# Linear attention segments: where the first products, the key turns and the small sample products stand in TensorE's hand-written order

## The chip, the core and the metric

The kernel runs on one core of one Trainium2 chip. The metric is the device time of one execution in microseconds (us). Before the change three timed executions took 1906.51, 1906.85 and 1907.57 us, median 1906.85.

## What is computed

One layer of a streaming encoder, for a prompt of 1024 rows and a sample of 32 rows with shared weights: an input projection, a gated linear attention (GLA), a banded softmax attention, a merge, a convolutional feed-forward part and a gated embedding. The change is in the GLA, which is in the reference

```python
b = jnp.cumsum(ai, axis=2)
decay = jnp.exp(jnp.where(mask, b[:, :, :, None, :] - b[:, :, None, :, :], -jnp.inf))
scores = jnp.einsum('bhic,bhjc,bhijc->bhij', qi, ki, decay)
o = (jnp.einsum('bhij,bhjv->bhiv', scores, vi)
     + jnp.einsum('bhic,bhcv->bhiv', qi * jnp.exp(b), S))
S = (jnp.exp(bl)[..., None] * S
     + jnp.einsum('bhjc,bhjv->bhcv', ki * jnp.exp(bl[:, :, None] - b), vi))
```

for 4 heads with keys of 128 and values of 256 columns, and for the sample from a given state.

## The kernel before

The GLA stage works through 16 **segments**, numbered u = 0 to 15: four per head, each of 256 prompt rows (two blocks of 128). The fourth segment of each head (u = 3, 7, 11, 15) also holds the 32 sample rows. The scores inside a block depend on the decay between two rows, so they are made in levels: level 0 pairs neighbours, level l pairs the two halves of runs of 2 to the l+1 rows, up to level 6, and a diagonal product gives the row with itself. On each level VectorE and ScalarE scale the keys and queries into tile `x`, TensorE multiplies them, and VectorE copies the valid part under a mask into `scores`.

TensorE, VectorE and ScalarE run in the order in which the code is written (a manual schedule); each engine stands until what its next instruction reads is there. Between the small GLA products TensorE has **filler**: the big projections of other heads, cut into units of 24 products of 352 columns (L818 to L820), and each unit into three pieces of 9, 9 and 6. `piece()` puts one piece into TensorE's order, `flush()` then has the finished unit copied out of PSUM, and the first piece of some units also splits the next weights into two halves on ScalarE and VectorE (L235, L236). `need` says after which segment an additional piece is given, so that the units last for the loop.

TensorE's order in one segment of the kernel before, with the lines of before:

- the diagonal products (L1256) and level 0 (L1263), the turn of the weighted keys (L1287, a transpose), one piece
- levels 1 and 2 (L1270, in the sample's segments each followed by the sample's product L1273), one piece
- the products that update the state (L1324, L1327), levels 3 and 4, the turn of the previous segment's outputs (L1408, L1412), one piece
- levels 5 and 6, two pieces
- the turn of the scores (L1278), one piece
- the outputs: old state and scores times values (L1347, L1348 with `scores`, L1348 with `turned`, and L1352, L1353 for the sample), then two or three pieces.

Beside it, the turns of the values (L1184) and the three decay products of the next head (L1064) are spread over the first three segments of a head. ScalarE copies the turned keys (L1292) before the state products can start; VectorE makes the masked copies (L1302, L1306, L1310), and the masked copy into `turned` (L1280) that the last output product reads. The diagonal products of the sample, its level products 1 to 4 and the diagonal products of the blocks are written into one PSUM tile, `dg`. All these products write one of six single PSUM banks.

Of the kernel before, what the change touches and what calls it, by code (L numbers as in the profile page):

```python
# [21 lines left out]
NS = 32  # L22
# [91 lines left out]
def emit(tc, a):  # L114
    nc = tc.nc
    ve, ac, po, pe, dma = nc.vector, nc.scalar, nc.gpsimd, nc.tensor, nc.sync
# [330 lines left out]
    for g, (n, c) in enumerate(PLE):  # L447
        s = chunk(c)
# [255 lines left out]
    B, HA, X, R, S = {}, {}, {}, {}, {}  # L704

    def blocks(t, m):
        return t.rearrange("p (n s) -> p n s", s=2 * m)
# [58 lines left out]
    fill = {"raw": {}, "w": {}, "at": 0, "load": 0, "split": 0, "now": None, "done": []}  # L766
# [26 lines left out]
    def gate_rows(n2):  # L793
        for n in (2 * n2, 2 * n2 + 1):
            GB[n] = tl(bo, [P, T], tag=f"gb{n}") if n2 else evt()
            dma.dma_start(GB[n], d_gb[n])
# [31 lines left out]
    def piece():  # L828
        if fill["now"] is None:
            if fill["at"] == len(units):  # L830
                return
            fill["now"] = unit_parts(*units[fill["at"]]), 0
        parts, n = fill["now"]
        next(parts)
        fill["now"] = (parts, n + 1) if n < 2 else None
        if n == 0:
            i, c = units[fill["at"]]
            if c < 2 and fill["split"] == i + 1 <= FIRST:
                split_half(c)
                if c:  # L840
                    load_tile()
        if n == 2:
            fill["at"] += 1

    def flush():
        for f in fill["done"]:
            f()
        fill["done"].clear()
# [278 lines left out]
    for i in range(len(WORK) + SK + 1):  # L1127
        g, j = divmod(i, NW)
# [14 lines left out]
        n = i - SK - 1  # L1143
# [29 lines left out]
    def head(h):  # L1173
        kq = tl(gp, [P, 2, T], tag="kq", bufs=2)
        HA.setdefault(h, {}).update({"kq": kq, "k": kq[:, 0], "q": kq[:, 1], "vt": tl(gp, [P, 9, 256], tag="vt", bufs=2)})

    def turn_values(h, n):
        g = HA[h]
        cnt = min(2, 9 - n)
        ps = ps_one()  # L1180
        w = P if n < 8 else NS
        for i in range(cnt):
            for j in range(2):
                pe.transpose(ps[:w, i * 256 + j * P : i * 256 + (j + 1) * P], g[f"v{j}"][:, (n + i) * P : (n + i) * P + w], ident)  # L1184
        ac.activation(g["vt"][:w, n : n + cnt], ps[:w, : cnt * 256].rearrange("p (i v) -> p i v", v=256), AF.Copy)

    def seg(u):
        h, s = divmod(u, 4)
        t0, nt = SEGS[s]
        return HA[h], h, s, t0, nt  # L1190
# [51 lines left out]
    def level_bank(u, l):  # L1242
        return R[u]["lo" if l < 4 else "hi"][:, 128 * (l % 4) : 128 * (l % 4) + 128]

    def level_products(u, between):
        g, h, s, t0, nt = seg(u)
        x, k, q, qo = X[u], g["k"], g["q"], g["qo"]
        r = R[u]
        r.update({"dg": ps_one(), "lo": ps_one(), "hi": ps_one()})
        dg = r["dg"]  # L1250
        cnt = (nt + P - 1) // P
        ns = [(t0 // P + i, i * P, P if i < 2 else NS) for i in range(cnt)]
        r["ns"] = ns
        for i, (n, o, w) in enumerate(ns):
            o, m = (P - o, n ^ 1) if i < 2 else (o, n)
            pe.matmul(dg[:w, o : o + w], k[:, n * P : n * P + w], q[:, m * P : m * P + w], start=True, stop=True)  # L1256

        def to(i, l, w):
            return level_bank(u, l)[:w, 64 * i : 64 * i + 64] if i < 2 else dg[:w, 288 + 16 * l : 304 + 16 * l]

        for i, (n, o, w) in enumerate(ns):
            m = n ^ 1 if i < 2 else n
            pe.matmul(to(i, 0, w), k[:, n * P : n * P + w], qo[:, m * 64 : m * 64 + w // 2], start=True, stop=True)  # L1263
        r["to"] = to
        for l in range(1, 7):
            if l == 4:
                score_copies(u, range(-1, 4))
            if l % 2:
                between[l // 2]()
            pe.matmul(level_bank(u, l), x[:, l - 1, 0:P], x[:, l - 1, P : 2 * P], start=True, stop=True)  # L1270
            if len(ns) > 2 and 2 << l <= NS:
                xs = x[:, l - 1, 256:nt]
                pe.matmul(to(2, l, NS), xs, blocks(xs, 1 << l)[:, :, 1 << l :], start=True, stop=True)  # L1273

    def score_turn(u):
        r = R[u]
# [5 lines left out]
    def key_turns(u):  # L1282
        g, h, s, t0, nt = seg(u)
        r = R[u]
        kp = r["kp"] = ps_one()
        for n, o, w in r["ns"]:
            pe.transpose(kp[:w, o : o + P], X[u][:, 6, o : o + w], ident)  # L1287
# [86 lines left out]
    def squares_a(u):  # L1374
        r = R[u]
        parts = parts_of(u)
        v = r["sums"] = tl(gp, [P, 3], tag="sums", bufs=2)
        t = r["t"] = tl(gp, [P, 3, 256], tag="ot", bufs=1)
        if len(parts) > 2:
            po.memset(v, 1.0)  # L1380
        for w, i, ps in parts:
            ac.activation(t[:w, i], ps, AF.Square, accum_out=v[:w, i : i + 1])
        v = v[:, : len(parts)]
        ve.tensor_scalar(v, v, 1.0 / 256, EPS, op0=ALU.mult, op1=ALU.add)
# [58 lines left out]
    to, of = [t.rearrange("p (s c j) -> p s c j", c=2, j=P) for t in (kq[:, 1, :NP], d_kq[1, :, :NP])]  # L1443
# [17 lines left out]
    piece()  # L1461
    turn_values(0, 6)
    turn_values(0, 8)
    while fill["at"] < 3 * 15:
        piece()
        flush()

# [18 lines left out]
    def steps_of(f, n):  # L1486
        for i in range(n):
            f()

    need = [fill["at"] + n / 30 for n in range(85, 85 * 12 + 1, 85)]  # L1490
    need += [3 * FIRST - (3 * FIRST - need[-1]) * n / 3 for n in (2, 1)]

    for u in range(16):
        h, s = divmod(u, 4)
        if s == 0:
            if h == 3:
                rows_times = branch_rows()
                next(rows_times, None)
            if h < 3:
                head(h + 1)  # L1500
                chain = decays(h + 1)
        flush()
        weight_sum(h, s, X[u][0:1, 0, 0:1])
        loads(u)
        if u < 15:
            differences(u + 1, range(1, 5))

        def turns():
            if s == 0 and h:
                turn_values(h, 0)  # L1510
            key_turns(u)
            piece()

        def states():
            piece()
            key_copies(u)
            if u:
                output_copies(u - 1)
            updates(u)

        def turn_back():
            if u:
                output_turns(u - 1)
            piece()

        level_products(u, (turns, states, turn_back))
        flush()
        if u < 15:
            exponentials(u + 1, (1, 2, 3, 4))
            flush()  # L1530
            exponentials(u + 1, (7, 6))
        if u == 15:
            flush()
        score_copies(u, range(4, 7))
        if u:
            results(u - 1)
        if u == 15:
            branch_split(1)
        flush()
        if u < 15:  # L1540
            differences(u + 1, (5,))
            factors(u + 1, (7, 1, 2))
        steps_of(piece, 2)
        score_turn(u)
        if s == 3:
            next(chain, None)
        if u < 15:
            factors(u + 1, (3, 4, 6))
            exponentials(u + 1, (5,))
        piece()  # L1550
        flush()
        if s < 2 and h:
            turn_values(h, 2 + 4 * s)
        outputs(u)
        if s == 3:
            next(chain, None)
        squares_a(u)
        if u < 15:
            factors(u + 1, (5,))
        else:  # L1560
            branch_split(2)
        if u >= 12:
            next(rows_times, None)
        flush()
        n = (5, 4, 2, 0)[s]
        steps_of(lambda: next(chain, None), n - n // 2)
        piece()
        if s < 2 and h:
            turn_values(h, 4 + 4 * s)
        steps_of(lambda: next(chain, None), n // 2)  # L1570
        piece()
        if u == 14:
            while fill["at"] < 3 * FIRST:
                piece()
                flush()
            xp.release()
            bo = pool("bo", side="right")
            for x in "hl":
                OB[x] = tl(bo, [P, 4, T], F32R, tag="b" + x)
            branch_split(0)  # L1580
            split_tile()
            load_tile()
            gate_rows(1)
        roots(u)
        if u < 14 and fill["at"] + (fill["now"] or (0, 0))[1] / 3 < need[u]:
            piece()
        if u == 13:
            next(rows_times, None)
            gate_rows(0)
    flush()  # L1590
    piece()
    flush()
# [47 lines left out]
    for n in range(KT):  # L1640
        hi, lo = weights(a["w_br_a"][n])
        g, t = evt(), evt()
# [4 lines left out]
        for c in range(NC):  # L1647
            s = chunk(c)
# [568 lines left out]
    X = {}  # L2217
# [580 lines left out]
```

## Time and profile before

| | before |
|---|---|
| median of three timed executions | 1906.85 us |
| profiled execution, its own time | 1907.61 us |
| its span, first to last instruction | 1905.9 us |
| TensorE busy (matmuls) | 1873.0 us, 98% |
| VectorE, ScalarE busy | 1231.1 us, 955.1 us |
| granted TensorE clock | 0.998 |
| the segments' loop in the trace | about 588 to 878 us |

The profiled execution is 0.76 us above the median. In the rows below, a product of two full float32 operands shows up as two records of each instruction, so `x4` is two instructions. A row's first number is its start; since products are pipelined, a record's own duration overlaps the next one, and what counts for the path is the distance from one start to the next.

### The profile page before, as it was taken

Reading aid. Unit: us, or ns where it says so; the run is one execution under the profiler, and the core shown is the slowest. Engines: PE = TensorE matmul, PEld = TensorE weight load, DVE = VectorE, ACT = ScalarE, POOL = GpSimd, SP = SyncE. Lnnn points to the kernel's source line nnn. Section 1 sums busy time; section 2 is a strip of 40 time slices with the busy share of each in tenths; the row PEclk is TensorE's granted clock in tenths of the full one; section 3 lists DMA queues with packets and bytes.
Section 4 is the critical chain, followed back from the end, with each engine's and each line's share of the span. In section 5 each row is a group of like instructions: output and inputs, shape, how many; then the busy total and the mean of one; then the engine's idle time right before and its main releaser. Section 6 shows DMA issues by size and latency. Waiting matters only on the chain.

```text
span 1905.9 us, 34520 instructions
## 1 busy us (share of the span) xinstructions
PE 1873.0 (98%) x13688; PEld 1835.0 (96%) x13688; DVE 1231.1 (65%) x2297; ACT 955.1 (50%) x2012; POOL 211.8 (11%) x374
## 2 busy tenths in 40 slices
PE   8999999999999999999999999999999999999996
PEld 7999999999999999999999999999999999999996
DVE  6955544566655666676444776777877775558776
ACT  7545335666666665653334544433343344555555
POOL 0000001010000111101210121111112110000112
PEclk9999999999999999999999999999999999999999
DMA  7223326233315556578633446344445568897746
GB/s 280 82 101 109 108 86 188 69 96 94 93 48 149 157 151 164 166 226 281 229 123 103 154 149 221 136 153 153 131 113 124 119 176 285 265 299 240 236 150 109
DMA packets 112191, 300.89 MB, mean 158 GB/s; under 512 B 12629, under 2 KB 35997, under 8 KB 111389
## 3 DMA queue, kind: packets, MB, share of 16 engines
q1 hardware_dynamic: 82572, 205.95, 34.1%
q0 software_dynamic: 28016, 88.05, 17.0%
q10 hardware_dynamic: 1440, 4.69, 0.6%
q8 instruction: 107, 1.75, 0.4%
q14 instruction: 56, 0.45, 0.1%
HBM read 201.20 MB, written 114.09 MB: 165 GB/s over the span
## 4 chain that ended last, share of the span: by engine, by line
PE 84%; DVE 6%; ACT 5%; DMA 3%; issue 2%; SPq 0%; ACTq 0%; DVEq 0%
PE two L2012 6%; PE two L2014 6%; PE two L2013 6%; PE mm L230 6%; PE mm L232 6%; PE mm L231 6%; PE mm L818 5%; PE mm L819 5%; PE mm L820 5%; PE two L618 4%; PE two L619 4%; PE two L620 4%; PE two L2474 3%; PE two L2473 3%; PE two L2472 3%
## 5 line engine op out<-in xcount | busy, mean ns | idle before, releaser
L818 PE MATMUL mm<-xh,whi 128*128 128x352 f32 x696 | 240.2, 345 | 0.0
L820 PE MATMUL mm<-xh,wlo 128*128 128x352 f32 x696 | 225.1, 323 | 0.0
L819 PE MATMUL mm<-xl,whi 128*128 128x352 f32 x696 | 224.6, 323 | 0.0
L2474 PE MATMUL two<-d,wlo 128*128 128x264 f32 x616 | 175.5, 285 | 0.5 <-DVE wlo L2211 0.5
L2473 PE MATMUL two<-d,whi 128*128 128x264 f32 x616 | 174.7, 284 | 0.8 <-DVE d L2162 0.8
L2472 PE MATMUL two<-d,whi 128*128 128x264 f32 x616 | 174.7, 284 | 0.3 <-ACT whi L2210 0.3
L2014 PE MATMUL two<-mh,wlo 128*128 128x264 f32 x576 | 163.2, 284 | 0.0
L2013 PE MATMUL two<-ml,whi 128*128 128x264 f32 x576 | 163.0, 284 | 0.0
L2012 PE MATMUL two<-mh,whi 128*128 128x264 f32 x576 | 161.7, 285 | 1.1 <-DVE gx L2024 1.1
L818 PEld LDWEIGHTS mm<-xh,whi 128*128 128x128 f32 x696 | 131.3, 189 | 4.0 <-issue 1.2
L819 PEld LDWEIGHTS mm<-xl,whi 128*128 128x128 f32 x696 | 131.3, 189 | 0.5
L820 PEld LDWEIGHTS mm<-xh,wlo 128*128 128x128 f32 x696 | 130.6, 188 | 0.0
L2473 PEld LDWEIGHTS two<-d,whi 128*128 128x128 f32 x616 | 115.8, 188 | 1.2 <-DVE d L2162 1.2
L2472 PEld LDWEIGHTS two<-d,whi 128*128 128x128 f32 x616 | 116.5, 189 | 0.6 <-ACT whi L2210 0.6
L2474 PEld LDWEIGHTS two<-d,wlo 128*128 128x128 f32 x616 | 115.5, 188 | 0.9 <-DVE wlo L2211 0.9
L2012 PEld LDWEIGHTS two<-mh,whi 128*128 128x128 f32 x576 | 107.5, 188 | 1.4 <-DVE gx L2024 1.4
L2014 PEld LDWEIGHTS two<-mh,wlo 128*128 128x128 f32 x576 | 108.5, 188 | 0.0
L2013 PEld LDWEIGHTS two<-ml,whi 128*128 128x128 f32 x576 | 108.4, 188 | 0.0
L955 ACT ACTIVATE s<-s,sm 128x640 f32<-128x640 f32 (+5 forms) x72 | 50.6, 703 | 93.4 <-DVE sm L954 93.4
L618 PE MATMUL two<-th,whi 128*128 128x264 f32 x320 | 90.8, 284 | 0.0
L619 PE MATMUL two<-tl,whi 128*128 128x264 f32 x320 | 90.8, 284 | 0.0
L620 PE MATMUL two<-th,wlo 128*128 128x264 f32 x320 | 90.6, 284 | 0.0
(630 smaller groups left out, 5881.3 us busy)
## 6 DMA issues: line engine op xcount, KB each, us to landing
raw<-in_w_in SPq DMA_DIRECT2D x52, 512.0 KB, 3.9
d_b<-av POOLq DMA_DIRECT2D x33, 528.0 KB, 3.5
d_ws<-in_w_down POOLq DMA_DIRECT2D x24, 704.0 KB, 6.6
uraw<-d_b SPq DMA_DIRECT2D x32, 528.0 KB, 4.3
raw<-in_w_up SPq DMA_DIRECT2D x27, 512.0 KB, 3.6
wraw<-d_ws SPq DMA_DIRECT2D x16, 704.0 KB, 5.8
d_b<-gc POOLq DMA_DIRECT2D x11, 792.0 KB, 4.8
sraw<-in_w_up SPq DMA_DIRECT2D x17, 512.0 KB, 4.6
```

The lines of the kernel that those rows point to most:

```text
L618: pe.matmul(ps[:, j, :HC], w[0][:, k], x[0](k, s), start=st, stop=False, skip_group_check=True)
L619: pe.matmul(ps[:, j, :HC], w[0][:, k], x[1](k, s), start=False, stop=False, skip_group_check=True)
L620: pe.matmul(ps[:, j, :HC], w[1][:, k], x[0](k, s), start=False, stop=sp_, skip_group_check=True)
L818: pe.matmul(ps, wh, h[:, k, s], start=(k == 0), stop=False)
L819: pe.matmul(ps, wh, l[:, k, s], start=False, stop=False)
L820: pe.matmul(ps, wl, h[:, k, s], start=False, stop=(k == cnt - 1))
L2012: pe.matmul(ps[:, j, :HC], w[0][:, k], x[0][:, k, s], start=st, stop=False, skip_group_check=True)
L2013: pe.matmul(ps[:, j, :HC], w[0][:, k], x[1][:, k, s], start=False, stop=False, skip_group_check=True)
L2014: pe.matmul(ps[:, j, :HC], w[1][:, k], x[0][:, k, s], start=False, stop=sp_, skip_group_check=True)
L2472: pe.matmul(o, wh, xh_[:, s], start=(k == 0 and p in (0, 4, 5)), stop=False, skip_group_check=True)
L2473: pe.matmul(o, wh, xl_[:, s], start=False, stop=False, skip_group_check=True)
L2474: pe.matmul(o, wl, xh_[:, s], start=False, stop=(k == HD - 1 and p in (3, 4, 6)), skip_group_check=True)
```

## The change

1. A new function `level_start(u)` holds the diagonal products and, for every segment but the first, the key turns. It is called for segment u+1 directly behind `outputs(u)`. Level 0 stays in `level_products`, in one group with levels 1 and 2; the function `turns` between them is gone, and its piece is the first of two pieces ahead of the state products.
2. One more filler unit is worked off ahead of the loop (`head(1)` comes earlier for this, since that unit belongs to head 1); the loop's `need` goes from 85 to 82 thirtieths per segment. The sum of the units is the same.
3. The sample's level products 1 to 4 stand in one group behind level 3, ahead of the masked copies.
4. Behind the last segment one more `flush` and `piece` stand ahead of the last output copies and turns.

```diff
+    def level_start(u):
+        g, h, s, t0, nt = seg(u)
+        k, q = g["k"], g["q"]
+        r = R.setdefault(u, {})
         r.update({"dg": ps_one(), "lo": ps_one(), "hi": ps_one()})
...
             pe.matmul(dg[:w, o : o + w], k[:, n * P : n * P + w], q[:, m * P : m * P + w], start=True, stop=True)
+        if u:
+            key_turns(u)
...
+        if s == 0 and h:
+            turn_values(h, 0)
...
+        if not u:
+            key_turns(u)
         for l in range(1, 7):
             if l == 4:
                 score_copies(u, range(-1, 4))
-            if l % 2:
-                between[l // 2]()
+            if l in (3, 5):
+                between[l // 2 - 1]()
             pe.matmul(level_bank(u, l), x[:, l - 1, 0:P], x[:, l - 1, P : 2 * P], start=True, stop=True)
-            if len(ns) > 2 and 2 << l <= NS:
-                xs = x[:, l - 1, 256:nt]
-                pe.matmul(to(2, l, NS), xs, blocks(xs, 1 << l)[:, :, 1 << l :], start=True, stop=True)
+            if l == 3 and len(ns) > 2:
+                for i in range(1, 5):
+                    xs = x[:, i - 1, 256:nt]
+                    pe.matmul(to(2, i, NS), xs, blocks(xs, 1 << i)[:, :, 1 << i :], start=True, stop=True)
...
-    while fill["at"] < 3 * 15:
+    head(1)
+    while fill["at"] < 3 * 15 + 1:
...
-    need = [fill["at"] + n / 30 for n in range(85, 85 * 12 + 1, 85)]
+    need = [fill["at"] + n / 30 for n in range(82, 82 * 12 + 1, 82)]
...
         outputs(u)
         if s == 3:
             next(chain, None)
+        if u < 15:
+            level_start(u + 1)
...
+    flush()
+    piece()
     flush()
     piece()
     flush()
     output_copies(15)
```

In the rows of the order below, `one` is a PSUM tile in a single bank and `mm` one of the filler's; `ident` marks a transpose, `ev` is a row tile of values, `x` the scaled keys and queries, `kt` and `ks` the turned keys, `vt` the turned values. Lines above L1244 are the same in both kernels; L1263 of before is L1273 of the change, L1270 is L1282, L1273 is L1286, L1287 is L1300, L1324 and L1327 are L1337 and L1340, L1347 and L1348 are L1360 and L1361, L1408 is L1421.

First place: TensorE at the head of the loop, from the last turn of values to the filler. Before:

```order
L1184 MATMUL one_6895<-ident_78,ev_6525 32x128
L1256 MATMUL one_6913<-kq_6779 128x128 x2
L1263 MATMUL one_6914<-qo_6858,kq_6779 128x64 x2
L1287 MATMUL one_6920<-ident_78,x_6798 128x128 x2
L818 MATMUL mm_6875<-xh_111,whi_6663 128x352
```

The change:

```order
L1184 MATMUL one_6895<-ident_78,ev_6525 32x128
L818 MATMUL mm_6875<-xh_111,whi_6663 128x352
...
L820 MATMUL mm_6875<-xh_111,wlo_6734 128x352
L1256 MATMUL one_6919<-kq_6779 128x128 x2
L1273 MATMUL one_6920<-qo_6858,kq_6779 128x64 x2
```

The rest of a begun unit, 15 filler products, now stands between the turn of the values and the first diagonal products.

Second place: TensorE from the outputs of segment 11 to level 0 of segment 12, the first of the last head. Before, behind the filler that follows the outputs:

```order
L820 MATMUL mm_9307<-xh_111,wlo_9156 128x352
L1256 MATMUL one_9381<-kq_8530 128x128 x2
L1263 MATMUL one_9382<-qo_9299,kq_8530 128x64 x2
L1184 MATMUL one_9388<-ident_78,ev_9161 128x128
L1184 MATMUL one_9388<-ident_78,ev_9369 128x128
```

The change:

```order
L1361 MATMUL one_9322<-vt_7712,turned_6775 128x256
L1365 MATMUL one_9214<-vt_7712,scores_s_6774 32x256
L1366 MATMUL one_9214<-ss_9178,x_8969 32x256
L1256 MATMUL one_9332<-kq_8544 128x128 x2
L1300 MATMUL one_9337<-ident_78,x_9180 128x128 x2
L818 MATMUL mm_9307<-xh_111,whi_9091 128x352
...
L820 MATMUL mm_9307<-xh_111,wlo_9166 128x352
L1184 MATMUL one_9389<-ident_78,ev_9171 128x128
L1184 MATMUL one_9389<-ident_78,ev_9377 128x128
```

The diagonal products and the key turns went ahead of the filler, and the turns of the values now follow directly on the last filler product of unit 9307.

Third place: TensorE in segment 3, the first with sample rows, from the sample's state product to the output turns. Before:

```order
L1327 MATMUL one_7538<-vt_6780,ks_7531 128x256
L1270 MATMUL one_7493<-x_7281 128x128
L1273 MATMUL one_7492<-x_7281 32x16
L1270 MATMUL one_7494<-x_7281 128x128
L1273 MATMUL one_7492<-x_7281 32x16
L1408 MATMUL one_7554<-ident_78,ot_7429 128x128 x4
```

The change:

```order
L1340 MATMUL one_7552<-vt_6780,ks_7545 128x256
L1282 MATMUL one_7455<-x_7322 128x128
L1286 MATMUL one_7454<-x_7322 32x16 x4
L1282 MATMUL one_7456<-x_7322 128x128
L1421 MATMUL one_7570<-ident_78,ot_7465 128x128 x4
```

All four sample products of the levels are one group now, and none stands behind level 4.

More of the change, by code (lines that the diff above doesn't have):

```diff
@@ L1243, in level_bank @@
         return R[u]["lo" if l < 4 else "hi"][:, 128 * (l % 4) : 128 * (l % 4) + 128]
-    def level_products(u, between):
+    def level_start(u):
         g, h, s, t0, nt = seg(u)
-        x, k, q, qo = X[u], g["k"], g["q"], g["qo"]
-        r = R[u]
+        k, q = g["k"], g["q"]
+        r = R.setdefault(u, {})
         r.update({"dg": ps_one(), "lo": ps_one(), "hi": ps_one()})
@@ L1256, in level_products @@
             pe.matmul(dg[:w, o : o + w], k[:, n * P : n * P + w], q[:, m * P : m * P + w], start=True, stop=True)
+        if u:
+            key_turns(u)
+    def level_products(u, between):
+        g, h, s, t0, nt = seg(u)
+        x, k, q, qo = X[u], g["k"], g["q"], g["qo"]
+        r = R[u]
+        dg, ns = r["dg"], r["ns"]
+        if s == 0 and h:
+            turn_values(h, 0)
         def to(i, l, w):
@@ L1488, in steps_of @@
             f()
-    need = [fill["at"] + n / 30 for n in range(85, 85 * 12 + 1, 85)]
+    need = [fill["at"] + n / 30 for n in range(82, 82 * 12 + 1, 82)]
     need += [3 * FIRST - (3 * FIRST - need[-1]) * n / 3 for n in (2, 1)]
+    level_start(0)
     for u in range(16):
@@ L1499, in emit @@
             if h < 3:
-                head(h + 1)
+                if h:
+                    head(h + 1)
                 chain = decays(h + 1)
@@ L1506, in emit @@
             differences(u + 1, range(1, 5))
[L1508 to L1512, printed above, removed]
         def states():
-            piece()
+            steps_of(piece, 2)
             key_copies(u)
@@ L1524, in turn_back @@
             piece()
-        level_products(u, (turns, states, turn_back))
+        level_products(u, (states, turn_back))
         flush()
```

## The prediction

> **What bounds the kernel now.** The page comes first: the span, the busy line and the chain that ended last.
>
> ```profile
> span 1905.9 us, 34520 instructions
> PE 1873.0 (98%) x13688; PEld 1835.0 (96%) x13688; DVE 1231.1 (65%) x2297; ACT 955.1 (50%) x2012; POOL 211.8 (11%) x374
> PE 84%; DVE 6%; ACT 5%; DMA 3%; issue 2%; SPq 0%; ACTq 0%; DVEq 0%
> ```
>
> TensorE (PE) is busy 98% of the span and carries 84% of the chain; VectorE and ScalarE have 35% and 50% to spare. So the change, which keeps all products, can only gain where PE stands, or where a product costs more than it must. I therefore read the loop (588 to 878) in the timeline of PE, from start to start, and then its waits. The timeline's columns are start, duration, engine, line, operation, tiles and count; idle time and its releaser stand in brackets. The head of the loop, and the same products one segment on:
>
> ```profile
> 588.11 0.61 PE L1256 MATMUL one<-kq 128*128 128x128 f32 x4
> 589.87 0.66 PE L1263 MATMUL one<-qo,kq 128*128 128x64 f32 x4 [1.16 <-DVE qo L1101]
> 590.73 0.41 PE L818 MATMUL mm<-xh,whi 128*128 128x352 f32 x1
> ...
> 605.40 0.61 PE L1256 MATMUL one<-kq 128*128 128x128 f32 x4
> 606.38 0.41 PE L818 MATMUL mm<-xh,whi 128*128 128x352 f32 x1
> ...
> 607.92 0.61 PE L1270 MATMUL one<-x 128*128 128x128 f32 x4
> 608.28 0.41 PE L818 MATMUL mm<-xh,whi 128*128 128x352 f32 x1
> 608.53 0.32 PE L819 MATMUL mm<-xl,whi 128*128 128x352 f32 x1
> ...
> 610.68 0.61 PE L1270 MATMUL one<-x 128*128 128x128 f32 x4
> 611.13 0.60 PE L1408 MATMUL one<-ident,ot 128*128 128x128 f32 x4
> ```
>
> From 606.38 to 607.92 stand nine filler products, .17 each with the dearer first one; within a piece I take .16.
>
> **Part 1: level 0, the diagonal and the key turns.**
>
> (a) *Head of the loop.* The diagonal products, level 0 and a key turn take 588.11 to 590.73 = 2.62, and the same take 605.40 to 606.38 = .98 in segment 1. The difference, **1.64**, is the wait for `qo`. In the change 15 filler products (15 x .16 = 2.4) stand ahead of them. Level 0, needed at about 588.5 before, is then needed at about 590.9, while `qo` let it start at 589.87: a spare of 1. Without this cover the 1.64 would stay.
>
> (b) *Joining level 0 with levels 1 and 2.* One filler group less lies between small groups. Levels 1 and 2 before filler take 607.92 to 608.28 = .36, but the first filler product then takes .25 (608.28 to 608.53) instead of .16: .45 in all. Levels 3 and 4, followed by other small products, take 610.68 to 611.13 = .45. A small float32 record is .11 either way, so the joining is worth **0**, and I take no price for it.
>
> (c) *What the pieces move.* The extra unit and `need` shift where the short pieces (6 products) and the weight splits fall. Two waits of before hang on that:
>
> ```profile
> 599.17 0.32 PE L820 MATMUL mm<-xh,wlo 128*128 128x352 f32 x1
> 599.58 0.30 PE L1278 MATMUL one<-ident,scores 128*128 128x128 f32 x1
> ...
> 634.15 0.59 PE L1347 MATMUL one<-state,x 128*128 128x256 f32 x2
> 634.58 0.59 PE L1348 MATMUL one<-vt,turned 128*128 128x256 f32 x2
> ...
> 707.06 0.59 PE L1347 MATMUL one<-state,x 128*128 128x256 f32 x2
> 707.90 0.70 PE L1348 MATMUL one<-vt,turned 128*128 128x256 f32 x2 [0.25 <-DVE turned L1280]
> ```
>
> The score turn of segment 0 starts .41 behind the last filler product instead of .16: **.25**, gone with 18 instead of 15 products ahead of it. The output product that reads `turned` takes .84 in segment 6 (707.06 to 707.90) where segment 2 takes .43. Everything that waited on that tile, in the view of L1348's line:
>
> ```profile
>   DVE turned L1280: 1.8, 5
> ```
>
> Five waits, 1.8 idle; some of it lies under the tail of the product before, and I take half, **.9**. In the change the short piece between score turn and outputs falls on segments 0, 1, 4, 8, 12 and 15; there either no weight split stands ahead of `turned` in VectorE's queue or four value turns stand between. So I expect the waits gone. Bounds: 0 (they turn up elsewhere) and 1.8.
>
> (d) *New waits.* At the head of segment 12 the value turns used to have the diagonal and level 0 ahead:
>
> ```profile
> 805.92 0.61 PE L1256 MATMUL one<-kq 128*128 128x128 f32 x4
> 806.12 0.46 ACT L714 ACTIVATE ev<-mm 128x352 f32<-128x352 f32 x1 [0.44 <-PE mm L820]
> 806.75 0.61 PE L1184 MATMUL one<-ident,ev 128*128 128x128 f32 x4
> ```
>
> ScalarE starts copying the just finished unit `ev` .20 after that filler group ended at 805.92, and is done at 806.58. Now the value turns, the second of which reads this row tile, stand directly behind the unit: the first can run (.11), the second stands until about .66 plus a little for the release. I take **-.6**, once (bounds -.4 and -.8); behind it stand level 0 and all of PE. In segment 15 a filler product needs a bank that VectorE reads at L800:
>
> ```profile
> 863.60 0.49 PE L1270 MATMUL one<-x 128*128 128x128 f32 x2
> ...
> 865.53 1.01 DVE L800 TENSOR_TENSOR ev<-mm,ev 128x352 f32<-128x352 f32 x2
> ...
> 866.18 0.41 PE L818 MATMUL mm<-bh,whi 128*128 128x352 f32 x1
> ```
>
> Half of the 1.01, to 866.04, is what it waits for: .14 to spare. The masked copies that hold VectorE up start with the last of the sample products 1 to 3, just after 863.60; from there to the filler product PE has 2.58. With the sample products in one group ahead of level 4, that stretch is about 2.1, and VectorE's chain is as long as before, 2.4: **-.3** (bounds 0 and -.6).
>
> The key copy on ScalarE now stands behind two pieces:
>
> ```profile
> 608.25 0.37 ACT L1292 ACTIVATE kt<-one 128x256 f32<-128x256 f32 x1
> 609.82 1.02 PE L1324 MATMUL one<-vt,kt 128*128 128x256 f32 x4
> ```
>
> It ends at 608.62, 1.2 ahead of the state products. With 18 filler products (2.9) there instead of 9, I cost it at 0; the gap is the cover, and it is the slow rival below.
>
> **Part 2: the extra unit ahead.** It moves work and adds none: 0. `head(1)` issues no DMA where it goes; SP's queue sees only one load of filler weights move one place against the stores of outputs, and POOL's order stays.
>
> **Part 3: the sample's level products**, in segments 3, 7, 11 and 15:
>
> ```profile
> 641.73 0.38 PE L1270 MATMUL one<-x 128*128 128x128 f32 x2
> 642.04 0.23 PE L1273 MATMUL one<-x 128*32 128x16 f32 x2
> 642.21 0.49 PE L1270 MATMUL one<-x 128*128 128x128 f32 x2
> 642.79 0.43 PE L818 MATMUL mm<-xh,whi 128*128 128x352 f32 x1
> 643.06 0.32 PE L819 MATMUL mm<-xl,whi 128*128 128x352 f32 x1
> ...
> 645.92 0.49 PE L1270 MATMUL one<-x 128*128 128x128 f32 x2
> 647.28 0.66 PE L1408 MATMUL one<-ident,ot 128*128 128x128 f32 x4
> ```
>
> Before: levels 1 and 2 with their sample products 641.73 to 642.79 = 1.06, the next filler product .27, .11 too long; levels 3 and 4 with theirs 645.92 to 647.28 = 1.36, in which the fourth sample product stands until VectorE has made the masked copy that reads its bank:
>
> ```profile
>   DVE scores L1302: 1.2, 4
> ```
>
> That is .3 of idle time in each of four segments. Sum: 2.53. After: levels 1 and 2 .45 and levels 3 and 4 .45 as above. A sample pair from start to next start is 642.21 - 642.04 = .17, so four are .66 at .165. Going over to the 32-column shape and back costs about .2: 641.73 to 642.04 is .31 where two records are .22, and 642.21 to 642.79 is .58 where .22 and .17 make .39. Sum: 1.76. Saving .77 x 4 = **3.1**. Not shown by any row is a record of this shape behind its like; by the nearest rows it lies between .05 and .11 (half a pair .085; a small full record .11): .95 and .52 a segment, 3.8 and 2.1 in all.
>
> By the Trainium skill, page "TensorE: Matmul & The Clock Gate", section "LDWEIGHTS (loading the stationary operand)", a weight load costs its columns over 1.2 ns: 107 ns for 128, which the .11 records here bear out, and 27 ns for 32, an estimate by which eight grouped records are .21 instead of .66.
>
> **Part 4: the end.**
>
> ```profile
> 877.04 0.32 PE L820 MATMUL mm<-bh,wlo 128*128 128x352 f32 x1
> 877.55 0.80 PE L1408 MATMUL one<-ident,ot 128*128 128x128 f32 x4 [0.19 <-ACT ot L1401]
> 878.28 0.31 PE L1412 MATMUL one<-ident,ot 32*128 32x32 f32 x2
> ```
>
> The last output turns start .51 behind the filler instead of .16, and then take .73 (877.55 to 878.28) where .55 would do: **.5** goes once 9 more products (1.5) stand ahead of them.
>
> **Sum.** 1.64 + .25 + .9 + 3.1 + .5 - .6 - .3 = 5.5. The profiled execution took 1907.61, so 1902.1 by its measure; it is .76 above the median 1906.85, so I forecast **1901.4**. About .2% (3.8) is what a measurement can tell from no change: faster means under 1903.0.
>
> **Rivals.**
>
> *The sample records are cheap in a group.* If the second record behind its like costs .05 and not .085, as the row at 642.04 cannot exclude, eight cost .4 or less, 1.0 to 1.4 more is saved, and the time is about **1900.1**. Against it: no small float32 record in these rows comes under .08. Chance .12. It is the case that the skill's rule just named would give.
>
> *The gain is eaten.* The `turned` waits reappear (-.9), sample records cost .11 (-1.0), the two new waits are at their dear ends (-.5), and something like .3 is lost elsewhere: 5.5 - 2.7 = 2.8, **1904.1**. For it: the loop is full of waits with .1 to .3 to spare (866.04 against 866.18), and every regrouping shifts them. Chance .20.
>
> *The order changes and the cost does not.* If a sample record costs its switch each time, wherever it stands, part 3 is 0 and the sum 2.4: **1904.5**. Against it: .3 of the stretch at 645.92 is a plain wait. Chance .06.
>
> *Slower: ScalarE's key copy comes late.* It is now queued behind a unit's evacuation (.46 as at 806.12) and whatever split the second piece brings. If these hold it until after the filler ahead of the state products, PE stands in each segment. It has 1.2 of spare and gains nine products of cover; it decides from a delay of some 2.7 on, and to end up slower than before .35 must be lost in each of 16. At .7 a segment, 11.2 - 5.5: **1912.5**. Against it: ScalarE is at 50%. Chance .07.
>
> **How the numbers follow.** The forecast has .50, these rivals .45, and .05 is for none of them. Low end: all terms at their top (1.64 + .25 + 1.3 + 3.8 + .5 - .4) = 7.1, about 1899.7. High end: 1.3 + .1 + 0 + 2.1 + .3 - .8 - .6 and .4 lost in places not seen = 2.0, about 1904.9; the slower rival is left out, with its .07. Faster: the forecast's .50 nearly whole, .12, and some of the rest: .70. Same: the two cases at 1904 to 1904.5, .23. Slower .07.
>
> **What would show it.** Right: no wait for `qo` at the loop's first level 0; eight sample records in one row group of about .66, with no wait for the masked copies; no idle time ahead of the products with `turned`; the output turns at the end without a wait on ScalarE; about .6 ahead of the value turns in segment 12 and .3 in segment 15. Wrong: waits on ScalarE's key copy ahead of the state products, waits on `turned` in other segments, or sample groups of over 1 us.

## The result and the profile after

| | before | after |
|---|---|---|
| median of eleven executions | 1907.57 us | 1903.40 us |
| ratio, 95% interval | | 0.9976 (0.9968 to 0.9984) |
| profiled execution, its own time | 1907.61 us | 1903.33 us |
| its span | 1905.9 us | 1901.6 us |

The change made the kernel 4.2 us faster by the medians, 3.1 to 6.1 by the interval; forecast were 5.5. The forecast time was 1901.4, with a range of 1899.7 to 1904.9, counted from the median of three executions, 1906.85; the eleven before have 1907.57, so .7 of the distance between 1901.4 and 1903.40 is the starting point. The forecast's mark for faster, under 1903.0, is missed by .4, while the change of 4.2 is just past the 3.8 that stood behind that mark. In a second set of eleven executions on another occasion the ratio was 0.9978 (0.9969 to 0.9987).

The page's span, busy line and chain line of after:

```profile
span 1901.6 us, 34524 instructions
PE 1870.8 (98%) x13688; PEld 1836.0 (97%) x13688; DVE 1231.2 (65%) x2297; ACT 956.2 (50%) x2012; POOL 211.1 (11%) x374
PE 85%; DVE 6%; ACT 5%; DMA 2%; issue 2%; POOL 0%; SPq 0%; ACTq 0%; DVEq 0%; POOLq 0%
```

The same products on the same bound: nothing else became the limit. The measure for all that follows is a stretch of TensorE's timeline, from the first turn of values ahead of the loop to the first product behind it. Its two ends before, and then after:

```profile
583.72 1.47 PE L1184 MATMUL one<-ident,ev 128*128 128x128 f32 x12
...
890.29 0.32 PE L230 MATMUL mm<-bh,whi 128*128 128x352 f32 x1
```

```profile
584.12 1.47 PE L1184 MATMUL one<-ident,ev 128*128 128x128 f32 x12
...
885.96 0.32 PE L230 MATMUL mm<-bh,whi 128*128 128x352 f32 x1
```

306.6 became 301.8: the stretch gained **4.7**, and the rest of the 4.3 between the two spans is a start that happened to come .4 later, in code that is the same. A second profile of the changed kernel gave 301.8 again, so this stretch tells differences of a tenth, where whole executions scatter by 2 to 3 us.

The waits of TensorE in the loop after (line, releaser; total, times, longest):

```profile
PE one L1184 <- ACT ev L714: 0.4, 1, 0.4
PE mm L818 <- ACT ev L714: 0.3, 1, 0.3
PE mm L818 <- DVE ev L800: 0.2, 1, 0.2
```

All three waits of before (for `qo`, for `turned`, for the last output copies) are gone, and three others came. The first and the third were forecast, the second was not. The timeline of TensorE after, at the head of the loop, in segment 1 and in segment 3:

```profile
590.94 0.61 PE L1256 MATMUL one<-kq 128*128 128x128 f32 x4
591.38 0.56 PE L1273 MATMUL one<-qo,kq 128*128 128x64 f32 x4
591.78 0.39 PE L1300 MATMUL one<-ident,x 128*128 128x128 f32 x2
592.00 0.61 PE L1282 MATMUL one<-x 128*128 128x128 f32 x4
592.37 0.41 PE L818 MATMUL mm<-xh,whi 128*128 128x352 f32 x1
...
608.43 0.55 PE L1273 MATMUL one<-qo,kq 128*128 128x64 f32 x4
608.83 0.66 PE L1282 MATMUL one<-x 128*128 128x128 f32 x4
609.24 0.41 PE L818 MATMUL mm<-xh,whi 128*128 128x352 f32 x1
...
641.53 0.71 PE L1282 MATMUL one<-x 128*128 128x128 f32 x4
642.00 0.41 PE L818 MATMUL mm<-xh,whi 128*128 128x352 f32 x1
...
646.10 0.49 PE L1282 MATMUL one<-x 128*128 128x128 f32 x2
646.51 0.42 PE L1286 MATMUL one<-x 128*32 128x16 f32 x8
646.87 0.49 PE L1282 MATMUL one<-x 128*128 128x128 f32 x2
647.20 0.60 PE L1421 MATMUL one<-ident,ot 128*128 128x128 f32 x4
```

Three things are to be seen. At the head, diagonal products, level 0 and key turns run without a gap, 590.94 to 592.00. The group of eight sample records takes 646.51 to 646.87 = .36, where .66 was forecast. And levels 1 and 2 directly behind level 0 take 608.83 to 609.24 = .41 in segment 1, but only .37 at 592.00, where the key turns stand between: the shape ahead costs something, and the forecast had put this at nothing. (The .47 at 641.53, in segment 3, come behind a record with 32 weight columns.)

The new waits, on TensorE, VectorE and ScalarE: at the head of segment 12, twice in segment 15, and ahead of the last output turns:

```profile
801.55 0.27 PE L1184 MATMUL one<-ident,ev 128*128 128x128 f32 x1
802.27 0.55 PE L1184 MATMUL one<-ident,ev 128*128 128x128 f32 x3 [0.45 <-ACT ev L714]
```

```profile
854.18 1.14 ACT L235 ACTIVATE whi<-raw 128x512 fp32r<-128x512 f32 x2
...
855.44 0.32 PE L820 MATMUL mm<-bh,wlo 128*128 128x352 f32 x1
855.55 0.45 ACT L714 ACTIVATE ev<-mm 128x352 f32<-128x352 f32 x1
...
856.05 0.43 PE L818 MATMUL mm<-bh,whi 128*128 128x352 f32 x1 [0.29 <-ACT ev L714]
```

```profile
861.21 0.60 PE L1282 MATMUL one<-x 128*128 128x128 f32 x4
861.42 0.95 DVE L800 TENSOR_TENSOR ev<-mm,ev 128x352 f32<-128x352 f32 x2
861.99 0.43 PE L818 MATMUL mm<-bh,whi 128*128 128x352 f32 x1 [0.18 <-DVE ev L800]
```

```profile
872.64 0.16 DVE L1408 SCALAR_TENSOR_TENSOR rs<-sums,y 128x3 f32<-128x3 f32 x1
872.72 1.01 DVE L800 TENSOR_TENSOR ev<-mm,ev 128x352 f32<-128x352 f32 x2
...
872.85 0.32 PE L820 MATMUL mm<-bh,wlo 128*128 128x352 f32 x1
...
873.30 0.43 PE L818 MATMUL mm<-bh,whi 128*128 128x352 f32 x1
...
874.87 0.60 PE L1421 MATMUL one<-ident,ot 128*128 128x128 f32 x4
```

By starts, against the same products undisturbed: the second value turn begins .72 behind the first instead of .11, and the third .17 behind the second (.66 in all); the filler product at 856.05 begins .61 behind its forerunner instead of .16, and the next .27 behind it (.56); the one at 861.99 is .42 late; the one at 873.30 comes .45 behind instead of .16, and the next .27 behind it (.40). In the second case ScalarE's evacuation (its copy of a finished unit out of PSUM), which frees the filler's bank, stands behind two weight splits (854.18 to 855.32) in ScalarE's queue. In the last VectorE's gate copy (L800, which takes a finished unit out of PSUM and multiplies it by the gate) frees the bank, and it stands behind the root steps, the small operations on the row sums that end with L1408. The output turns at 874.87 wait for nothing; the nine products that were to cover their wait do.

### The profile page after: what moved, and what is told of

It is laid out like the page before. It is cut to its first block, busy times and chain, and to the rows that moved or that the text cites. A ratio compares the mean times of both kernels' runs of the same rounds, so it can differ in the third digit from the quotient of the medians.

```text
span 1901.6 us, 34524 instructions
## 1 busy us (share of the span) xinstructions
PE 1870.8 (98%) x13688; PEld 1836.0 (97%) x13688; DVE 1231.2 (65%) x2297; ACT 956.2 (50%) x2012; POOL 211.1 (11%) x374
## 4 chain that ended last, share of the span: by engine, by line
PE 85%; DVE 6%; ACT 5%; DMA 2%; issue 2%; POOL 0%; SPq 0%; ACTq 0%; DVEq 0%; POOLq 0%
PE two L2026 6%; PE two L2027 6%; PE two L2028 6%; PE mm L230 6%; PE mm L232 6%; PE mm L231 5%; PE mm L818 5%; PE mm L820 5%; PE mm L819 5%; PE two L2487 4%; PE two L2488 4%; PE two L2486 4%; PE two L618 4%; PE two L619 4%; PE two L620 4%
```

## The experiments

Twelve runs, in three groups. Expected and measured figures are for the stretch, 306.6 before and 301.8 after.

**Each part alone.** `samples_alone` puts only the sample products of part 3 into the kernel before:

```diff
-            if len(ns) > 2 and 2 << l <= NS:
-                xs = x[:, l - 1, 256:nt]
-                pe.matmul(to(2, l, NS), xs, blocks(xs, 1 << l)[:, :, 1 << l :], start=True, stop=True)
+            if l == 3 and len(ns) > 2:
+                for i in range(1, 5):
+                    xs = x[:, i - 1, 256:nt]
+                    pe.matmul(to(2, i, NS), xs, blocks(xs, 1 << i)[:, :, 1 << i :], start=True, stop=True)
```

> Only part 3: the kernel before with the sample's level products 1 to 4 in one group behind level 3. Measured on TensorE from the first value turn ahead of the loop to the first product behind it (306.6 us before). Theory: a record of this shape behind its like costs about .03, the group of eight about .36, whatever stands around it; .74 of waits and 2.8 of records go, and the wait of a filler product in segment 15 on the gate copies (about .4) appears: 303.5. Rival, the forecast's record price of .085: the group .66, four segments 3.1 less .3: 303.8 and the group's row tells. Rival, the group is cheap only together with the moved level 0: group .66 or more.

Measured: 302.9, ratio to before 0.9978 (0.9970 to 0.9987). The timeline of TensorE in segment 3:

```profile
644.70 0.49 PE L1270 MATMUL one<-x 128*128 128x128 f32 x2
645.12 0.42 PE L1274 MATMUL one<-x 128*32 128x16 f32 x8
645.48 0.49 PE L1270 MATMUL one<-x 128*128 128x128 f32 x2
645.80 0.60 PE L1409 MATMUL one<-ident,ot 128*128 128x128 f32 x4
```

The group is .36 (645.12 to 645.48) with level 0 where it was: both rivals fall. Levels 3 and 4 take 644.70 to 645.80 = 1.10 instead of 1.36, levels 1 and 2 .36 instead of 1.06, and the records behind them are .07 shorter: 1.03 a segment, 4.1 in four. The wait of .42 for L800 in segment 15 came along; 4.1 - .4 = 3.7, measured 3.65. The expectation's own sum of 3.5 was somewhat low.

`order_alone` has part 1 only:

```diff
+    level_start(0)
...
-        level_products(u, (turns, states, turn_back))
+        level_products(u, (states, turn_back))
...
+        if u < 15:
+            level_start(u + 1)
```

> Only part 1: diagonal products and key turns behind the outputs, level 0 joined with levels 1 and 2, two pieces together; sample products and units as before. Same stretch, 306.6 before. Theory: joining is worth nothing; the wait for qo at the head of the loop stays (1.6) as do the waits for turned (about 1.0), and two waits come: the value turns at the head of segment 12 on ScalarE (.66) and a filler product early in segment 15 on ScalarE's evacuation (.56): 307.8, slower than before. Rival, each filler group less saves .1: 16 segments, 306.2 with the two waits.

Measured: 308.2, ratio 1.0012 (1.0003 to 1.0021). Slower, as expected, but of the two waits only that of .66 came, and 1.6 is too much for it alone. Its waits for `qo`, for `turned` and at the end are those of before, but behind the wait for `qo` two records of levels 1 and 2 in segment 0 take .21 each instead of .11, which is .2 more and which the changed kernel does not have. What is left, about **.77**, is no wait: where level 0, with its 64-column output, is followed by level 1, the first record of level 1 takes .165; where a transpose follows, .115. In eleven segments that is .6; the other .2 is spread in small differences that I could not assign one by one. The rival, that fewer filler groups save something, falls.

`unit_alone` has part 2 only:

```diff
+    head(1)
-    while fill["at"] < 3 * 15:
+    while fill["at"] < 3 * 15 + 1:
...
-    need = [fill["at"] + n / 30 for n in range(85, 85 * 12 + 1, 85)]
+    need = [fill["at"] + n / 30 for n in range(82, 82 * 12 + 1, 82)]
...
-                head(h + 1)
+                if h:
+                    head(h + 1)
```

> Only part 2: one more filler unit ahead of the loop and need 82 instead of 85. Same stretch, 306.6 before. Theory: the wait for qo (1.62), for the score turn of segment 0 (.25) and the waits for turned (.96) are a matter of where the pieces fall, and all go without part 1: 303.8. Rival, the waits for turned go only through the moved diagonal products and key turns: 304.7. Rival, the head's wait needs both: 306.6 to 305.5.

Measured: 303.8, ratio 0.9985 (0.9976 to 0.9994). The one wait of TensorE left in the loop, where before had three:

```profile
PE one L1408 <- ACT ot L1401: 0.2, 1, 0.2
```

So 2.8 us, more than half of the net gain, come from where the pieces fall, with no product regrouped. Both rivals fall.

`end_alone` has part 4 only (`flush()` and `piece()` once more behind the loop):

> Only part 4: one more flush and piece ahead of the last output copies. Same stretch, 306.6 before. Theory: the output turns' wait goes (.56), but the first filler product of the added piece waits for VectorE's gate copy, which is queued behind the root steps: .40 back, 306.4. Rival, the forecast's: the nine products cover it and .5 is gained: 306.1.

Measured: 306.4, ratio 0.9999 (0.9990 to 1.0008). The timeline at the end of the loop:

```profile
877.32 0.32 PE L820 MATMUL mm<-bh,wlo 128*128 128x352 f32 x1
877.76 0.43 PE L818 MATMUL mm<-bh,whi 128*128 128x352 f32 x1
878.03 0.32 PE L819 MATMUL mm<-bl,whi 128*128 128x352 f32 x1
```

The filler product comes .44 behind its forerunner, not .16: a cover that waits itself. Of .56 gained .40 is given back.

The four parts alone make -3.65 + 1.63 - 2.82 - .15 = -5.0; together they made -4.7. Two things that were seen make most of the difference: the wait of .56 that no part has alone, which the next run takes up, and the .2 of `order_alone` behind its wait for `qo`, which goes with that wait. They give -4.6.

`samples_as_before` is the changed kernel without part 3 (the first diff of this section undone):

> The changed kernel without part 3: each sample product behind its level as before. Same stretch, 301.8 in the changed kernel. Theory: 4.1 of part 3 are lost again, but the waits of .56 and .42 in segment 15 go with them, since both came of TensorE running ahead by the .7 and .5 that the group saves there: 305.0, and no wait on ScalarE's evacuation early in segment 15. Rival, the two pieces behind one another make that wait: it stays, 305.5.

Measured: 304.9, ratio 0.9994 (0.9985 to 1.0002). All that is left in the loop's waits:

```profile
PE one L1184 <- ACT ev L714: 0.4, 1, 0.4
```

Both waits of segment 15 are gone with the group, so the rival falls: two pieces behind one another do not make the wait by themselves. This fits that TensorE arrives there earlier by the time that the group saves. The wait of .56 needs the pieces too, since `samples_alone`, which has the group without them, does not show it. The price of the end piece, .40, stays.

**What a sample record costs.** `samples_twice` issues the group twice, the second time into a part of a bank that level 4 overwrites, so the outputs stay:

```diff
+                for i in range(1, 5):
+                    xs = x[:, i - 1, 256:nt]
+                    pe.matmul(level_bank(u, 4)[:NS, :16], xs, blocks(xs, 1 << i)[:, :, 1 << i :], start=True, stop=True)
```

> The changed kernel with the group of four sample products issued twice, the second time into a part of a bank that level 4 overwrites afterwards; 128x32 weights, 16 moving columns, eight records more in each of four segments. Stretch from the first value turn to the first product behind the loop, 301.8 us in the changed kernel. Theory: a record behind its like costs .03: .26 a segment, 302.9. Rival, the forecast's .085 is the price and the group of .36 has another reason: 304.6.

Measured: 302.6. Eight records more cost .25 in each segment, .03 apiece; the sum is 1.0, less .25 by which the wait of .42 in segment 15 got shorter. `wide_weights` adds the four products with 128 weight columns instead of 32:

```diff
+                for i in range(1, 5):
+                    pe.matmul(level_bank(u, 4)[:, :16], x[:, i - 1, 0:P], blocks(x[:, i - 1, 256:nt], 1 << i)[:, :, 1 << i :], start=True, stop=True)
```

> The changed kernel with four products more in the sample group, which take the 128-column blocks of x as weights and the same 16 moving columns, into a part of a bank that level 4 overwrites afterwards. Same stretch, 301.8 in the changed kernel. Theory: the weight columns set the price of a record, .11 with 128 of them: 8 x .11 = .9 a segment, 305.4. Rival, the 16 moving columns set it, .03 as in the group: .26 a segment, 302.9.

Measured: 305.0. The timeline of TensorE in segment 3, the changed group and the added one behind it:

```profile
648.34 0.43 PE L1286 MATMUL one<-x 128*32 128x16 f32 x8
648.70 1.06 PE L1288 MATMUL one<-x 128*128 128x16 f32 x8
649.61 0.47 PE L1282 MATMUL one<-x 128*128 128x128 f32 x2
```

Eight records .36 with 32 weight columns, .91 (648.70 to 649.61) with 128, the same 16 moving columns in both. So the width of the weights, and with it the number of output rows, sets the price of these small products, and the moving columns do not: the records with 128 of both cost .11 too. (Of the .36, .11 is the last record, ahead of a wider weight.) The four groups cost 3.6 more by this; the wait of .42 in segment 15 is gone for it, which leaves the 3.2 measured. The Trainium skill, page "TensorE: Matmul & The Clock Gate", section "LDWEIGHTS (loading the stationary operand)", states the time of a weight load by itself: columns over 1.2 ns, so 27 and 107 ns for 32 and 128 columns, an estimate. The trace agrees, with .03 and .11 from start to start; that this is the whole price of such a product is what the rows show. The prediction's .21 for eight grouped records, worked out from it, falls short of the .36 mostly by the first and the last record, which take .05 and .11.

Both kernels took far longer as a whole than the stretch tells, 1911.9 and 1912.8 us in one execution each. So the first ran again, timed:

> The kernel with the sample group issued twice once more, timed: its single look was 8.5 us above the changed kernel, of which .8 lay in the stretch. Theory: the rest belonged to that one execution (waits on transfers in stages whose code is unchanged), and it takes 1 to 2 us more than the changed kernel. Rival, 32 products more cost elsewhere in every execution: again 7 or more above the changed kernel, in the same stages.

Measured: 302.6 in the stretch, but 1909.25 us in the median, ratio to before 1.0011 (1.0002 to 1.0020). The theory falls: the 5 to 6 us outside the stretch are there again, in the same place. The changed kernel's repeat on the same chip:

> The changed kernel once more, beside the mended one on the same chip: both theories 301.8 in the stretch and a ratio to before of .9968 to .9984 as on record; it only shows how far executions and profiles of one kernel differ.

Measured: 1903.1 us, 301.8 in the stretch. Where the two part is told in the last section.

**Mending it.** `keys_behind_level0` moves the key turns between level 0 and level 1:

```diff
-        if u:
-            key_turns(u)
...
-        if not u:
-            key_turns(u)
+        key_turns(u)
```

> The changed kernel with the key turns put between level 0 and level 1, in all segments; the diagonal products stay behind the outputs. Same stretch, 301.8 in the changed kernel. Theory: the first record of level 1 costs .165 behind the 64-column records of level 0, .11 behind a turn, and a turn behind them .115: .055 in 15 segments, 301.0. Rival, the .055 is paid whatever follows level 0, or reappears ahead of the filler: 301.8. If ScalarE's key copy is late, a wait ahead of the state products shows it.

Measured: 301.0, ratio 0.9970 (0.9958 to 0.9982). TensorE's timeline in segment 1:

```profile
608.10 0.55 PE L1271 MATMUL one<-qo,kq 128*128 128x64 f32 x4
608.49 0.39 PE L1297 MATMUL one<-ident,x 128*128 128x128 f32 x2
608.71 0.61 PE L1279 MATMUL one<-x 128*128 128x128 f32 x4
609.08 0.41 PE L818 MATMUL mm<-xh,whi 128*128 128x352 f32 x1
```

Levels 1 and 2 are back at .37. The .8 that the stretch gained are .5 of this kind, though, and .3 from a shorter wait in segment 15 (the filler product comes .38 instead of .61 behind its forerunner); that the total hits the theory is partly luck. No wait for ScalarE's key copy came up.

`waits_taken_out` moves four places:

```diff
-        if s == 0 and h:
-            turn_values(h, 0)
...
             if l == 4:
+                if u == 15:
+                    flush()
                 score_copies(u, range(-1, 4))
+            if l == 3 and s == 0 and h:
+                turn_values(h, 0)
...
             branch_split(0)
+            flush()
             split_tile()
...
+        if u == 15:
+            flush()
         roots(u)
```

> The changed kernel with four places moved: value turns at a head's first segment behind level 2 instead of ahead of level 0; behind the 14th segment's rest the finished unit is evacuated ahead of the weight split; in segment 15 a gate copy ahead of the first masked copies; in segment 15 gate copies ahead of the root steps. Same stretch, 301.8 in the changed kernel. Theory: the waits of .66, .56 and .40 go, and some .2 of the .42: 300.0. Rival, the queues of ScalarE and VectorE are as long as before and each wait only goes to another tile: 301.0 or more, with new waits on the state products, the scores or the output turns.

Measured: 299.8, ratio 0.9970 (0.9957 to 0.9982). No wait of TensorE is left in the loop; all of the .42 went, not half. The rival falls: ScalarE and VectorE do as much work as before, and only its order mattered.

`both_mended` has both:

> The four moved places and the key turns between level 0 and level 1 together, everything else as in the changed kernel. Stretch from the first value turn to the first product behind the loop, 301.8 in the changed kernel, 299.8 with the four places, 301.0 with the key turns. Theory: of the .8 of the key turns about .5 were the shape and .3 a shorter wait that is gone already, so 299.3, and the execution some 2.5 below the changed kernel. Rival, the two share more: 299.8.

Measured: 299.3, ratio 0.9968 (0.9957 to 0.9978), median 1901.0 us beside 1903.1 of the changed kernel on the same chip. In the stretch it is 2.6 better than the change and 7.3 better than before; in whole executions the difference of 2.1 to the change is near what the scatter hides. `waits_taken_out` (one of its six executions took 1906.5, the others 1899.1 to 1901.4) and `keys_behind_level0` have overlapping intervals with it, so which of the three is best is told by the stretch alone.

## Why the prediction was right, and where it was not

The sign, the bound and most places held: the forecast had 5.5, the stretch shows 4.7. But the sum is that close since errors of both signs met. By its terms:

| term | forecast | measured |
|---|---|---|
| (a) wait for `qo` at the loop's head | +1.64 | +1.6 |
| (b) joining level 0 with levels 1 and 2 | 0 | -.77 |
| (c) score turn of segment 0 | +.25 | +.25 |
| (c) waits for `turned` | +.9 | +1.0 |
| (d) value turns in segment 12 | -.6 | -.66 |
| (d) gate copy in segment 15 | -.3 | -.42 |
| evacuation early in segment 15 | not seen | -.56 |
| part 3, sample products | +3.1 | +4.1 |
| part 4, the end | +.5 | +.16 |
| sum | 5.5 | 4.7 |

The value of (b) is what `order_alone` leaves when its waits are taken off; the others were read off rows or runs.

- **(a) and (c)** held in place and size; `unit_alone` shows that all three are a matter of where the pieces fall, as the forecast put it. It booked them under part 1, though, and part 2 at 0: by the runs part 2 alone is worth 2.8, and part 1 alone costs 1.6. The waits for `turned` are gone by little: in segments 4 and 8, where the forecast counted on the value turns, VectorE ends the copy .05 ahead of the product that reads it, no more than in the segments that waited before.
- **(d)** held: both waits stand where they were named, the second .1 dearer. That the shorter sample group brings the second on is shown by `samples_alone`, which has it, and `samples_as_before`, which has not.
- **(b) failed.** The forecast put the joining at 0: it compared levels 1 and 2 ahead of filler with levels 3 and 4 between small products and found .45 for both. Neither row has a 64-column product ahead. Before, level 0 stood behind the diagonal products and ahead of a transpose, a pair that the regrouping broke up. The rows of `keys_behind_level0`, which puts a transpose there again, give .5 of it back; .2 of it is not assigned.
- **Part 3 was mis-sized** by the price of a record behind its like: .085 was taken as half of a pair, .03 is measured. In the pair at 642.04 the second record's start to the next was the change to a wider weight, not its own price. The profile before could have told: the pair lasts .23 from its first start to its last end, and the view of L1273 gives .18 to .20 for one record, so the second began only .05 behind the first. That is the rival "the sample records are cheap in a group", and its mechanism was the true one; its time of 1900.1 did not follow, for (b), the unseen wait and part 4 took more than that back.
- **Part 4 failed at the word "cover".** Nine filler products do cover the output turns, but the first of them needs a bank that VectorE frees behind the root steps. The forecast had asked what the output turns wait for, not what the cover waits for.
- **The unseen wait** has a like cause. With two pieces one behind the other and the sample products gone from between, TensorE reaches the next unit's bank .56 before ScalarE, behind two weight splits, has evacuated it. The forecast looked at what ScalarE's queue does to the key copy, which never was late, and not at the evacuation in the same queue.

The rival "the gain is eaten" had its time, 1904.1, nearer to the median than the forecast's 1901.4. Of its four causes two did not come (waits for `turned`, records of .11), the two forecast waits were dearer by .2 in all, and the "something like .3 lost elsewhere" was 1.7: (b), the unseen wait and what part 4 lacks. The rival "the order changes and the cost does not" falls by the group's .36, and the one on the slow side, a late key copy, did not come up in any run.

## What to carry to other kernels

When a wait is to be covered by moving independent work ahead of it, look up what that work itself waits for: here .40 of the .56 gained at the end and nearly 1 of the 4.1 of the sample products went back to filler whose bank was not free. Here small products were cheaper when grouped by the width of their weights, and a 64-column product cost less when a transpose followed it; both come out of the distances from start to start, which a merged row of several records hides. And where TensorE is the bound and other engines are half idle, the order inside their queues still counts: moving four places in them took out every wait in the loop, with no work left out.

## What the runs showed that was not expected

Eight more records in each of four segments, 1 us of work, cost the whole kernel 6 us (1909.25 against 1903.1 us, same chip). The stretch has .8 of it; nearly all of the rest lies in a later stage whose code is the same, between 1314 and 1342 us. There ScalarE writes the tile `gc` anew and stands until the last write of it to memory, on GpSimd's queue, has landed. The row in the changed kernel, repeated, and in `samples_twice_again`:

```profile
1327.59 1.27 ACT L1877 ACTIVATE gc<-gx,vec 128x1058 f32<-128x1058 f32 x1 [4.21 <-DMA d_b<-gc]
```

```profile
1331.05 1.27 ACT L1880 ACTIVATE gc<-gx,vec 128x1058 f32<-128x1058 f32 x1 [7.20 <-DMA d_b<-gc]
```

That write took 4.7 us from issue to landing in the one and 6.5 in the other, and the write of the tile before it 7.8 and 9.1. The same two writes took 5.8 to 6.4 and 8.6 to 9.0 in the single executions of `wide_weights` and `samples_twice`, and 4.5 to 4.7 and 7.6 to 8.0 in all eleven profiles of kernels with the original number of products, though some of those reach the stage 3 us earlier and others nearly 7 us later. Behind ScalarE's row TensorE waits for weights and tiles (`whi`, `wlo`, `gx`), three times between 1332 and 1336.3 and 3.0 us longer in all than in the changed kernel.

Then something follows that is no wait: the clock that TensorE is granted falls. The view of the next 6 us in the changed kernel, repeated, and in `samples_twice_again` gives the length, the busy time and records of PE, PEld, DVE, ACT and POOL, then the granted clock, the share of the DMA engines and GB/s:

```profile
1336.00:1342.00 6.00, 6.00 (x52) 6.00 (x51) 4.94 (x9) 2.59 (x4) 0.77 (x1) 1.00 0.81 266
```

```profile
1336.00:1342.00 6.00, 5.70 (x26) 5.70 (x27) 5.47 (x12) 1.84 (x4) 1.79 (x4) 0.51 0.37 135
```

TensorE gets through half as many products there, .22 apart instead of .12, which costs another 2.4 us. In `samples_twice` the clock was .54 from 1340 to 1343; in `wide_weights`, where the first of the three waits is shorter (.2 instead of .9 and .7, then .9 and 1.5 in all three), it stayed at 1.00. Why the writes land later with 32 products more, far ahead of them, and which idle time brings the clock down, stays open.
